# A convolution with max pooling on one core: turned weight taps as neighbours in one row, joint maxima and copies of two images over one PSUM tile, first casts on ScalarE, a last step in two row groups, and a new order

## The chip, the core and the metric

The kernel runs on one core of a Trainium2 chip. The time is the device time of one execution in microseconds, as the median over several runs. A profile of one execution gives the span from the first to the last instruction and what each engine did in it. Engines are named as the profile names them: PE (TensorE), DVE (VectorE), ACT (ScalarE), POOL (GpSimd), SP (SyncE).

## What is computed

`x` is 16 images of 64 channels of 64 x 64 float32 values, `weight` is 128 x 64 x 3 x 3. The result is the 3 x 3 convolution with padding of one pixel, followed by the maximum over each 2 x 2 square:

```python
x_pad = np.pad(x, ((0, 0), (0, 0), (1, 1), (1, 1)))
conv[b, co] += weight[co, ci, kh, kw] * x_pad[b, ci, kh:kh+64, kw:kw+64]   # over ci, kh, kw
output[b, c, i, j] = np.max(conv[b, c, 2*i:2*i+2, 2*j:2*j+2])              # 16 x 128 x 32 x 32
```

## The kernel before

**Work.** Two images lie side by side on the 128 partitions (64 channels each). A step is one pair of images and a quarter of the output rows: 8 output rows of 64 columns before the maximum over columns, for both images, so 32 steps in all (`TYPES`, line 37). Image `h` (0 or 1) of a step uses partitions 64h to 64h+63 on the input side, so the products of image 0 and image 1 use the two row halves of the PE array and run side by side. One product is three matmuls (the taps `kw` = 1, 0, 2, function `taps`, lines 188 to 209) of up to 64 x 512 elements into one of eight PSUM accumulators of 512 float32 values per partition, which is one bank (line 61). A product of image 0 is always interleaved with a product of image 1 (`lanes`, lines 251 to 259): three matmuls of each, in turn. This text calls such a group of six matmuls a slot.

**Two kinds of step.** With c0 and c1 the convolution of an even and the following odd row, each step forms a part that both share and takes the maximum of the rest, so that the maximum over rows is taken before the shared part is added. A K step has five products: PA1 and PA2 into accumulator `ta`, PB1 and PB2 into `tb`, PR (the shared part) into `tb` after the maximum. A W step has four: P2 and P0 into `ta`, P3 into `tb`, P1 (shared) into `tb` after the maximum. A W step starts `tb` from a copy of `ta` (SE, line 404).

**What the other engines do for a step.** Per image: EV (line 395) copies `ta` out of PSUM to SBUF on ACT, MX (line 425) puts the maximum of `tb` and that copy back into `tb` on DVE, then the shared product is added by PE, OD (line 429) copies the odd columns of `tb` to SBUF on ACT, CM (line 433) takes the maximum of the even columns and that copy on DVE and frees `tb`. After the second image's CM a store of both images is issued on SP. Of a W step, D (line 337) and mostly E (line 328) are row differences on POOL, WS (line 310) is a row sum on DVE; KS (line 297) is that of a K step. L and LK load input.

**Order.** The order of every instruction is written out by hand in the string `ORDER` (lines 493 to 547): `MX.4.1` is MX of step 4, image 1. Each engine works through its own instructions in that order. A tile framework puts semaphore waits between engines wherever one instruction reads or writes what another writes or reads. The queues are in order: an instruction that waits holds all that stand behind it on its engine.

**The start.** The weights arrive as [128, 576] and are cast and combined into slots of 64 columns of `wq` (g0, g1, g2, D0, D2, GS, GM, GP). PE turns each two neighbouring slots into one 128 x 128 block (`turn`, T...), and a copy brings the blocks from PSUM to `wt` (`turn_out`, V...). Seven groups have four slots each with a zero or a copied slot (`ring`, u..., on POOL) between, 25 turns in all (lines 133 to 186). The first rows of x are cast on DVE (XEa, XOa, XEb, XOb, line 450). The first K step and first W step run in row halves (F.k.part and G.k.part; Ea, Eb on DVE, Da, Db on POOL make the differences for G). Eight matmuls on a constant (line 551) stand at the very start.

**The end.** The last step, 31, is a W step. Its two images are stored apart, one on ACT's queue and one on SP's (lines 443 to 445).

Of the kernel before, what the change touches and what calls it, by code (L numbers as in the profile page):

```python
# [11 lines left out]
def kernel(  # L12
# [25 lines left out]
    DIFF_ON_VECTOR = (3, 4, 6, 11,)  # L38
    CAST_ON_VECTOR = ()
    SUM_BY_REDUCTION = (1, 3, 9, 11, 12, 14, 16, 17, 19, 20, 22,)  # L40
# [9 lines left out]
    d_pool = ctx.enter_context(tc.tile_pool(name="d_pool", bufs=5))  # L50
    e_pool = ctx.enter_context(tc.tile_pool(name="e_pool", bufs=5))
# [3 lines left out]
    od_pool = ctx.enter_context(tc.tile_pool(name="od_pool", bufs=6))  # L55
    o_pool = ctx.enter_context(tc.tile_pool(name="o_pool", bufs=6))
# [4 lines left out]
    acc = [psum.tile([128, R, W], FP32, name=f"acc_{i}") for i in range(8)]  # L61
# [5 lines left out]
    sbuf_op = [None]  # L67

# [64 lines left out]
    BLOCKS = {"D2": 1, "G0": 5, "D0": 9, "G2": 13, "GM": 17, "G1": 21, "GP": 25}  # L133
    D2, G0, D0, G2, GM, G1, GP = BLOCKS.values()
    RING = ("GM", "G1", "GP")
    wq = const.tile([CO, 29, CI], BF16)
    wt = const.tile([128, 28, CO], BF16)
    gsum = const.tile([CO, 3, CI], FP32)
    for s in range(0, GM, 4):
        nc.gpsimd.memset(wq[:, s, :], 0.0)  # L140
# [8 lines left out]
    def ring(m):  # L149
        s = BLOCKS[m]  # L150
        nc.gpsimd.tensor_copy(out=wq[:, s + 3, :], in_=wq[:, s, :])  # L151

    def turned_cols(m):
        lo = BLOCKS[m] - (m not in RING)
        hi = BLOCKS[m] + 3
        tp = acc[turned[m]].rearrange("p a b -> p (a b)").bitcast(BF16)
        return lo, hi, tp[:, 0 : (hi - lo) * CO]
# [12 lines left out]
    def turn_out(m):  # L170
        free.append(turned[m])
        lo, hi, src = turned_cols(m)
        dst = wt[:, lo:hi, :].rearrange("p a b -> p (a b)")
        if m == "GM":
            nc.scalar.mul(dst, src, 0.5)
        elif m == "GP":
            nc.vector.tensor_scalar_mul(out=dst, in0=src, scalar1=0.5)
        elif m in ("G0", "G2"):
            nc.scalar.copy(out=dst, in_=src)
        else:  # L180
            nc.vector.tensor_copy(out=dst, in_=src)

    def tap_of(m0, kw, half):
        if m0 in (GM, G1, GP):
            return m0 + (kw - half) % 3
        return m0 + kw - half

    def taps(t, h, m0, rows, start=False, skip=None, span=(0, R)):
# [7 lines left out]
        def one(kw):  # L196
            o0, o1, c0, c1 = (0, W, 0, W) if kw == 1 else (1, W, 0, W - 1) if kw == 0 else (0, W - 1, 1, W)
            if start and kw == 1:
# [3 lines left out]
                wt[lo : lo + CI, tap_of(m0, kw, h), :],  # L202
# [18 lines left out]

    def take(where, s, h, fresh=True):
        t = next((t for t in free if fresh or t not in unset), free[0])
        free.remove(t)
        where[s, h] = t
        return t

# [162 lines left out]
    def late_load(s):  # L390
        behind(wload(s), sbuf_op[0])

    ev, od, ot, made = {}, {}, {}, {}

    def evac(s, h):
        ev[s, h] = ev_pool.tile([128, R, W], FP32, name="ev")
# [31 lines left out]

    def odd(s, h):
        od[s, h] = od_pool.tile([128, R, WO], FP32, name="od")  # L430
        nc.scalar.copy(out=od[s, h], in_=acc[tb[s, h]][:, :, 1::2])  # L431

    def colmax(s, h):
        if s not in ot:
            ot[s] = o_pool.tile([128, 2, R, WO], FP32, name="o")
        t = tb.pop((s, h))
# [3 lines left out]
        p, q = place[s]  # L440
        dst = out[2 * p : 2 * p + 2, :, q * R : (q + 1) * R, :].rearrange("b c h w -> c b (h w)")
        src = ot[s].rearrange("p b h w -> p b (h w)")
        if s == N - 1:
            store = nc.scalar if made[s] == 1 else nc.sync
            store.dma_start(out=dst[:, h : h + 1], in_=src[:, h : h + 1])
        elif made[s] == 2:
            nc.sync.dma_start(out=dst, in_=src)


    def cast_rows(lo, hi):  # L450
        on_vector(nc.vector.tensor_copy(out=kx[0][:, lo:hi:2, :], in_=kfirst[:, lo:hi:2, :]))  # L451

    def cast_more(first):
# [15 lines left out]
        "XOa": lambda: cast_rows(1, kmid),  # L469
        "XOb": lambda: cast_rows(kmid, khi),  # L470
        "XEa": lambda: cast_rows(0, kmid),
        "XEb": lambda: cast_rows(kmid + 1, khi),
# [10 lines left out]
        "KS": ks, "WS": ws, "E": we, "D": wd, "L": wload, "LB": late_load, "LK": lk,  # L483
        "SE": seed, "EV": evac, "MX": rowmax, "OD": odd, "CM": colmax,
    }
    for m in BLOCKS:
        steps["u" + m] = lambda m=m: ring(m)
        steps["T" + m] = lambda m=m: turn(m)
        steps["V" + m] = lambda m=m: turn_out(m)
    for m in PRODUCTS:  # L490
# [3 lines left out]
        D0 g2 g1 TD0 TG2 g0 D2 XEa PR.0.1 TD2 VG2 PA1.2.1 VD0 TG0 uG1 TG1 GS F.2.0 VD2 XOa LB.3 LB.4 LB.6  # L494
        LB.8 LB.9 GM VG0 F.3.0 XOb F.0.0 uGM F.1.0 VG1 F.0.1 TGM PA2.2.1 XEb LK.0.0 F.1.1 F.2.1 F.3.1 VGM GP
        Ea KS.0 Eb EV.0.1 G.0.0 EV.0.0 G.0.1 uGP P2.3.1 SEa.0 SEa.1 SEb.1 MX.0.1 Da Db TGP SEb.0 MX.0.0 VGP
        LK.0.1 X2 PR.0.0 G.1.0 X1 G.2.0 PB1.2.1 PB2.2.1 WS.1 G.2.1 G.1.1 L.11 P0.3.1 PA1.2.0 PA2.2.0 P3.3.1
        OD.0.0 OD.0.1 EV.1.0 KS.2 E.3 CM.0.1 EV.1.1 P1.1.1 D.3 CM.0.0 PR.2.1 PB1.2.0 P2.3.0 MX.1.0 PB2.2.0
        EV.2.1 P1.3.1 SE.3.1 EV.2.0 WS.3 MX.1.1 P1.1.0 SE.3.0 P0.3.0 MX.2.0 MX.2.1 EV.3.1 PR.2.0 EV.3.0 D.4
        MX.3.1 OD.2.0 PA1.5.1 OD.1.0 E.4 PA1.5.0 PA2.5.0 P3.3.0 OD.1.1 OD.2.1 L.12 L.14 PA2.5.1 OD.3.1  # L500
        P2.4.1 CM.1.1 CM.2.0 P2.4.0 CM.1.0 PA1.7.1 D.6 EV.5.0 CM.3.1 CM.2.1 MX.3.0 PA2.7.1 PB1.5.1 SE.4.0
        PA1.7.0 PA2.7.0 EV.5.1 SE.4.1 EV.7.0 PB2.5.1 P0.4.1 P0.4.0 P2.6.1 KS.7 E.6 P3.4.1 WS.4 WS.6 P1.3.0
        EV.4.0 PR.5.1 KS.5 WS.8 EV.7.1 P0.6.1 PB1.5.0 PB1.7.0 PB2.5.0 PB2.7.0 L.16 P1.4.1 EV.4.1 MX.5.1
        P3.4.0 OD.3.0 SE.6.1 MX.5.0 LK.1.0 LK.1.1 CM.3.0 MX.4.1 P3.6.1 OD.5.1 PB1.7.1 MX.7.0 PB2.7.1 PR.5.0
        OD.5.0 P2.6.0 EV.6.1 E.8 PR.7.0 MX.4.0 OD.4.1 OD.7.0 CM.5.1 D.8 P1.4.0 SE.6.0 OD.4.0 CM.5.0 E.9
        MX.6.1 CM.7.0 CM.4.0 P1.6.1 P2.8.0 CM.4.1 D.9 P2.8.1 SE.8.0 P0.6.0 P2.9.1 MX.7.1 P3.6.0 OD.6.1
        EV.6.0 P0.8.0 L.17 P3.8.0 SE.8.1 CM.6.1 PR.7.1 EV.8.0 OD.7.1 P0.8.1 MX.6.0 SE.9.1 E.11 MX.8.0 P1.6.0
        D.11 CM.7.1 P2.9.0 OD.6.0 EV.8.1 CM.6.0 WS.9 P3.8.1 P1.8.0 P0.9.1 PA1.10.1 SE.9.0 P2.11.0 OD.8.0
        L.19 L.20 P3.9.1 PA2.10.1 KS.10 EV.9.1 SE.11.0 P0.9.0 CM.8.0 E.14 P2.11.1 MX.9.1 P3.9.0 MX.8.1
        P0.11.0 EV.9.0 EV.10.1 MX.9.0 P1.9.1 D.14 E.12 P1.8.1 PA1.10.0 P3.11.0 PA2.10.0 SE.11.1 OD.9.1  # L510
        P1.9.0 P2.14.0 WS.11 CM.9.1 P0.11.1 P3.11.1 EV.11.0 EV.11.1 OD.8.1 OD.9.0 EV.10.0 P1.11.0 PA1.13.0
        PA1.13.1 MX.11.0 MX.11.1 PA2.13.1 D.12 L.22 L.23 PA2.13.0 P2.12.0 CM.8.1 CM.9.0 D.16 P1.11.1 EV.13.1
        P2.12.1 OD.11.0 SE.14.0 OD.11.1 PB1.10.1 WS.14 P0.14.0 CM.11.0 PB2.10.1 P3.14.0 CM.11.1 L.24 P0.12.0
        SE.12.1 P0.12.1 SE.12.0 P3.12.1 P3.12.0 EV.14.0 PB1.10.0 P2.14.1 WS.12 PB2.10.0 EV.13.0 MX.10.1
        EV.12.1 MX.14.0 E.16 EV.12.0 MX.12.1 PR.10.1 P1.14.0 MX.12.0 SE.14.1 OD.10.1 P1.12.0 PB1.13.1
        PA1.18.0 KS.15 KS.13 CM.10.1 P0.14.1 MX.10.0 OD.14.0 P3.14.1 CM.14.0 EV.14.1 P1.12.1 PR.10.0
        PB2.13.1 WS.16 MX.13.1 PA2.18.0 PA1.15.1 PA2.15.1 PR.13.1 OD.10.0 MX.14.1 PB1.13.0 OD.12.1 EV.18.0
        LK.2.0 P1.14.1 PB2.13.0 P2.16.0 CM.10.0 L.25 PA1.15.0 OD.12.0 EV.15.1 OD.13.1 CM.12.1 PA2.15.0
        SE.16.0 CM.13.1 P0.16.0 CM.12.0 L.27 L.28 P3.16.0 MX.13.0 P2.16.1 D.17 PR.13.0 PB1.15.0 PB1.15.1
        E.17 D.20 E.20 D.19 PB2.15.1 PB2.15.0 SE.16.1 EV.15.0 WS.17 P0.16.1 MX.15.1 P3.16.1 EV.16.0 OD.14.1  # L520
        PR.15.1 P2.17.1 MX.16.0 P1.16.0 EV.16.1 OD.13.0 MX.16.1 OD.15.1 SE.17.1 CM.14.1 P1.16.1 P2.20.1
        CM.13.0 CM.15.1 OD.16.0 PA1.21.0 P2.17.0 MX.15.0 P0.17.1 PR.15.0 E.23 E.19 CM.16.0 P3.17.1 OD.16.1
        CM.16.1 SE.20.1 EV.17.1 P0.20.1 P3.20.1 WS.20 PA2.21.0 P2.19.0 OD.15.0 SE.17.0 P3.17.0 EV.20.1
        MX.17.1 CM.15.0 P1.17.1 E.24 P0.17.0 WS.22 PA1.21.1 SE.19.0 P0.19.0 OD.17.1 EV.21.0 MX.20.1 CM.17.1
        D.22 EV.17.0 PA2.21.1 EV.21.1 EV.19.0 P3.19.0 P2.19.1 MX.17.0 KS.18 P2.23.0 P1.17.0 WS.19 P1.20.1
        PA1.18.1 P0.19.1 SE.19.1 MX.19.0 PB1.18.0 OD.17.0 OD.20.1 PA2.18.1 PB2.18.0 EV.19.1 P1.19.0 CM.20.1
        D.23 CM.17.0 MX.18.0 E.22 P3.19.1 PB1.18.1 SE.23.0 P2.20.0 EV.18.1 MX.19.1 PB2.18.1 PR.18.0 P1.19.1
# [66 lines left out]
```

## Time and profile before

| what | value |
|---|---|
| median of 3 runs | 104.69 us (104.35 to 105.06) |
| the profiled execution's own time | 105.15 us |
| span of that execution | 103.4 us |
| outside the span | 1.75 us |
| busy: PE, DVE, ACT, POOL | 97.2, 92.0, 82.2, 75.6 us |
| first weight turn on PE, first product on PE | 4.40 us, 6.46 us |
| first matmul of PR.29, the third slot from the end | 96.13 us |
| last matmul of all begins | 98.30 us |
| last store is issued | 99.82 us |
| mean granted PE clock | 0.993 |

The profiled execution took 0.46 us more than the median of the runs, so a time that is summed against the profile is brought to the median by taking 0.46 us off. Busy time of PE counts pipelined matmuls, whose ends are modelled; the starts of the matmuls are the better clock. In a steady stretch a slot of six matmuls takes 0.645 us from its first start to the next slot's first start (PR.0.0 begins at 11.025 us, the next slot at 11.670 us).

### The profile page before, as it was taken

What the parts mean: (1) busy time and instruction counts of PE and PEld (TensorE: products, weight loads), DVE (VectorE), ACT (ScalarE), POOL (GpSimd) and SP (SyncE); (2) the same over time, 40 slices, a digit from 0 to 9 for tenths busy, and PEclk for the clock granted to TensorE, in tenths of its full rate; (3) what the DMA queues carried; (4) which work ended last, traced back from release to release, by engine and by line L of the source; (5) the groups of instructions that cost most, each with busy time, mean ns of one, the idle gap of its engine ahead of it and who ended that gap; (6) DMA issues with size and microseconds to landing.
All of it is one profiled execution on the core that took longest, in us unless ns stands there. A gap on an engine that the chain in (4) does not pass through costs nothing.

```text
span 103.4 us, 2541 instructions
## 1 busy us (share of the span) xinstructions
PE 97.2 (94%) x909; PEld 62.9 (61%) x909; DVE 92.0 (89%) x179; ACT 82.2 (79%) x181; POOL 75.6 (73%) x65
## 2 busy tenths in 40 slices
PE   6999799999999999999999999999999999999910
PEld 2497655555865465576666685556746777777600
DVE  1389899999999999999999999999989996979960
ACT  4546988886789997993887898987899898698820
POOL 6046869773995899998999997959997919970000
PEclk9999999999999999999999999999999999999997
DMA  2988999999999999999859992187699232006152
GB/s 62 299 312 262 360 291 268 349 416 404 248 194 298 286 318 339 351 340 204 163 159 261 312 384 101 56 205 263 176 154 257 81 136 101 0 13 233 65 202 102
DMA packets 13341, 23.33 MB, mean 226 GB/s; under 512 B 1040, under 2 KB 9488, under 8 KB 13328
## 3 DMA queue, kind: packets, MB, share of 16 engines
q1 hardware_dynamic: 12320, 20.68, 60.8%
q0 software_dynamic: 864, 2.36, 13.7%
q8 instruction: 7, 0.11, 0.4%
q10 hardware_dynamic: 144, 0.13, 0.4%
q14 instruction: 6, 0.05, 0.1%
HBM read 17.14 MB, written 8.39 MB: 247 GB/s over the span
## 4 chain that ended last, share of the span: by engine, by line
PE 91%; DVE 3%; issue 1%; DVEq 0%
PE acc L200 85%; PE acc L551 3%; PE acc L164 2%; DVE acc L427 2%; DVE o L437 1%; DVEq L589 0%; DVEq L437 0%; DVEq L427 0%
## 5 line engine op out<-in xcount | busy, mean ns | idle before, releaser
L200 PEld LDWEIGHTS <-wt 64*128 64x128 bf16 x876 | 59.6, 94 | 31.5 <-issue 1.5
L341 POOL TENSOR_TENSOR wd<-wx 128x1024 bf16<-128x1024 f32 x20 | 47.1, 2361 | 7.7 <-PE acc L200 3.4
L200 PE MATMUL acc<-wd,wt 64*128 64x504 bf16 (+3 forms) x264 | 50.1, 367 | 0.0
L200 PE MATMUL acc<-kx,wt 64*128 64x504 bf16 (+6 forms) x288 | 50.0, 356 | 0.0
L427 DVE TENSOR_TENSOR acc<-acc,ev 128x512 f32<-128x512 f32 x64 | 42.0, 691 | 1.1 <-ACT ev L401 0.3
L200 PE MATMUL acc<-we,wt 64*128 64x512 bf16 (+2 forms) x132 | 31.7, 367 | 0.0
L200 PE MATMUL acc<-ws,wt 64*128 64x504 bf16 (+1 forms) x126 | 28.7, 377 | 0.1
L401 ACT ACTIVATE ev<-acc 128x512 f32<-128x512 f32 x42 | 25.1, 608 | 2.7 <-PE acc L200 2.3
L431 ACT COPY od<-acc 128x256 f32<-128x256 f32 x64 | 22.5, 379 | 5.8 <-PE acc L200 5.2
L437 DVE TENSOR_TENSOR o<-acc,od 128x256 f32<-128x256 f32 x64 | 24.5, 416 | 2.1 <-ACT od L431 1.9
L411 ACT COPY acc<-acc 128x512 f32<-128x512 f32 x40 | 23.0, 581 | 3.0 <-PE acc L200 1.7
L332 POOL TENSOR_TENSOR we<-wx 128x512 bf16<-128x512 f32 x16 | 20.2, 1273 | 3.3 <-DVE ws L323 2.4
L200 PE MATMUL acc<-ks,wt 64*128 64x504 bf16 (+1 forms) x66 | 16.5, 377 | 0.5 <-DVE acc L427 0.5
L315 DVE TENSOR_REDUCE ws<-wx 128x512 bf16<-128x1024 f32 x11 | 13.5, 1229 | 0.0
L399 ACT COPY ev<-acc 128x512 f32<-128x512 f32 x22 | 12.9, 595 | 0.6 <-PE acc L200 0.6
L323 DVE TENSOR_TENSOR ws<-wx 128x512 bf16<-128x512 f32 x10 | 7.1, 723 | 0.0
L301 DVE TENSOR_TENSOR ks<-kx 128x512 bf16<-128x512 bf16 x11 | 4.6, 429 | 0.3 <-ACT kx L458 0.3
L551 PE MATMUL acc<-const-bfloat16-1.0 128*128 128x512 bf16 x8 | 3.6, 628 | 0.8 <-PEq L575 0.8
L95 POOL DMA_DIRECT2D kx<-in_x_dram x6 | 3.5, 587 | 0.7 <-DVE kx L451 0.7
L164 PEld LDWEIGHTS <-wq 128*128 128x128 bf16 x25 | 2.3, 132 | 1.4 <-issue 1.4
L151 POOL COPY wq<-wq 128x64 bf16<-128x64 bf16 x3 | 0.7, 241 | 3.1 <-ACT wq L462 2.5
L164 PE MATMUL acc<-ident,wq 128*128 128x128 bf16 x25 | 2.8, 285 | 0.0
(30 smaller groups left out, 22.3 us busy)
## 6 DMA issues: line engine op xcount, KB each, us to landing
out_dram<-o SPq DMA_DIRECT2D x31, 256.0 KB, 4.2
wx<-in_x_dram SPq DMA_DIRECT2D x10, 512.0 KB, 7.2
wx<-in_x_dram SPq DMA_DIRECT2D x5, 544.0 KB, 7.6
wx<-in_x_dram SPq DMA_DIRECT2D x5, 480.0 KB, 7.4
kx<-in_x_dram POOLq DMA_DIRECT2D x2, 528.0 KB, 7.4
ksecond<-in_x_dram SPq DMA_DIRECT2D x1, 512.0 KB, 7.0
kx<-in_x_dram POOLq DMA_DIRECT2D x2, 256.0 KB, 7.0
kx<-in_x_dram POOLq DMA_DIRECT2D x1, 496.0 KB, 12.0
```

The costliest lines, as they stand in the source:

```text
L164: nc.tensor.transpose(tp[:, (j - lo) * CO : (j - lo + 1) * CO], wq[:, j : j + 2, :].rearrange("a b c -> a (b c)"), ident,)
L200: nc.tensor.matmul(acc[t][:, i0:i1, o0:o1], wt[lo : lo + CI, tap_of(m0, kw, h), :], rows(lo, i0, i1, c0, c1), start=start and kw == 1, sto ...
L315: nc.vector.tensor_reduce(out=row["ws", s], in_=t[:, f : f + 2 * R, :].rearrange("p (r two) w -> p r w two", two=2), axis=mybir.AxisListTy ...
L323: nc.vector.tensor_tensor(out=row["ws", s], in0=t[:, f : f + 2 * R : 2, :], in1=t[:, f + 1 : f + 2 * R : 2, :], op=ADD)
L332: inst = (nc.vector if vector else nc.gpsimd).tensor_tensor(out=row["we", s], in0=t[:, f : f + 2 * R : 2, :], in1=t[:, f + 1 : f + 2 * R : ...
L341: nc.gpsimd.tensor_tensor(out=row["wd", s], in0=t[:, f + 1 : f + 1 + 2 * R, :], in1=t[:, f - 1 : f - 1 + 2 * R, :], op=SUB)
L399: nc.scalar.copy(out=ev[s, h], in_=acc[t])
L401: nc.scalar.mul(ev[s, h], acc[t], -1.0)
L411: nc.scalar.copy(out=acc[t], in_=acc[ta[s, h]])
L427: nc.vector.tensor_tensor(out=t, in0=t, in1=ev[s, h], op=MAX)
L431: nc.scalar.copy(out=od[s, h], in_=acc[tb[s, h]][:, :, 1::2])
L437: nc.vector.tensor_tensor(out=ot[s][:, h], in0=acc[t][:, :, 0::2], in1=od[s, h], op=MAX)
```

## The change

**Taps in one row.** `wq` has 25 slots and `wt` 24 blocks. The order of the groups is D0, G2, D2, G0, G1, GM, GP with no slot between the first five, so that a block that turns the last slot of one group turns the first slot of the next one too. 24 turns; no copied slots (`ring` is gone).

**Joint operations of two images.** All eight accumulators become one PSUM tile `bank` of eight banks. For steps in three lists, one instruction covers both images, through the view `bank[:, a : b + 1 : b - a]` of the two banks a and b. MM is the joint MX, OO the joint OD, CC the joint CM. Where image 0's bank has the higher number the joint form falls back to two single ones.

**First casts** XEa, XEb, XOa, XOb move from DVE to ACT; VG1 goes from DVE to ACT; VG2 and VGM from ACT to DVE. The late loads wait for the last cast.

**The last step** adds its shared product in two row groups (Z.0, Z.1), copies and maxes each group and image by itself (OZ.part.image, CZ.part.image) and stores each group for both images on SP's queue.

**Order and buffers.** `ORDER` is written anew. `d_pool` goes from 5 to 4 buffers, `e_pool` from 5 to 6, `od_pool` 6 to 4, `o_pool` 6 to 5; `ev2_pool` (3), `od2_pool` (3) and `last_pool` (4) are new. Which steps take their difference on DVE and their row sum by a reduction changes, their numbers (4 and 11) do not.

```diff
-    DIFF_ON_VECTOR = (3, 4, 6, 11,)
+    DIFF_ON_VECTOR = (3, 9, 16, 22,)
+    SWAPPED = ("VG1", "VG2", "VGM", "XEa", "XEb", "XOa", "XOb",)
+    JOINT_ROWMAX = (0, 1, 10, 11, 30,)
+    JOINT_ODD = (1, 2, 3, 5, 8, 10, 11, 14, 15, 27, 29, 30,)
+    JOINT_COLMAX = (0, 1, 2, 5, 8, 11, 12, 15, 21, 24, 29, 30,)
...
-    acc = [psum.tile([128, R, W], FP32, name=f"acc_{i}") for i in range(8)]
+    bank = psum.tile([128, 8, R, W], FP32, name="bank")
+    acc = [bank[:, i] for i in range(8)]
...
-    BLOCKS = {"D2": 1, "G0": 5, "D0": 9, "G2": 13, "GM": 17, "G1": 21, "GP": 25}
+    BLOCKS = {"D0": 1, "G2": 4, "D2": 7, "G0": 10, "G1": 13, "GM": 17, "GP": 21}
...
+    def both(s):
+        a, b = tb[s, 0], tb[s, 1]
+        return bank[:, a : b + 1 : b - a]
...
+    def rowmax_both(s):
+        if tb[s, 0] > tb[s, 1]:
+            rowmax(s, 0)
+            rowmax(s, 1)
+            return
+        nc.vector.tensor_tensor(out=both(s), in0=both(s), in1=ev2[s], op=MAX)
...
+    def odd_both(s):
+        if tb[s, 0] > tb[s, 1]:
+            odd(s, 0)
+            odd(s, 1)
+            return
+        od_tile(s, 0)
+        od_tile(s, 1)
+        nc.scalar.copy(out=od2[s], in_=both(s)[:, :, :, 1::2])
...
+    def colmax_both(s):
...
+        nc.vector.tensor_tensor(out=ot[s], in0=both(s)[:, :, :, 0::2], in1=od2[s], op=MAX)
+        free.extend((tb.pop((s, 0)), tb.pop((s, 1))))
+        store(s)
...
+    def last_product(part):
+        s = N - 1
+        m0, of = (GP, "ws") if TYPES[s] == "W" else (G1, "ks")
+        pair_of_taps(tb, s, m0, step1(row[of, s]), False, None, span_of(part))
...
+    def cast_rows(name, lo, hi):
+        dst, src = kx[0][:, lo:hi:2, :], kfirst[:, lo:hi:2, :]
+        if name in SWAPPED:
+            gate[0] = nc.scalar.copy(out=dst, in_=src)
+        else:
+            gate[0] = on_vector(nc.vector.tensor_copy(out=dst, in_=src))
```

The start and the end of the new order, and a piece of it (`...` marks what is left out):

```
D0 g2 g0 TD0 g1 D2 GS VD0 TG2 TD2 XEa TG0 VG2 TG1 XOa LB.3 ... F.2.0 XOb VG0
F.0.0 F.0.1 GM XEb GP KS.0 F.1.0 TGM F.1.1 EV.0.0 LK.0.0 VGM Ea F.3.0 F.2.1 Eb F.3.1 ...
VG1 Da G.0.0 G.0.1 MM.0 SEa.0 SEa.1 Db X1 TGP VGP G.1.0 G.2.0 SEb.1 SEb.0 ...
...
P2.3.0 PB1.2.0 EV.2.1 EV.2.0 MM.1 PB1.2.1 PB2.2.1 PB2.2.0 L.11 WS.3 SE.3.0 P1.1.0 P1.1.1 E.4 MX.2.1
MX.2.0 SE.3.1 P0.3.1 P0.3.0 OO.1 P3.3.0 P3.3.1 CC.1 E.6 D.4 EV.3.1 PR.2.0 ...
...
P0.31.1 EV.31.0 P3.31.1 PR.29.0 EV.31.1 MX.31.0 P1.30.0 P1.30.1 MX.31.1 OO.29
OO.30 CC.29 Z.0 Z.1 OZ.0.1 OZ.1.1 CC.30 OZ.1.0 CZ.0.1 OZ.0.0 CZ.1.0 CZ.1.1 CZ.0.0
```

In the built program, counting the increments of each semaphore tells which instruction a wait is for. The joint operations whose two banks are not neighbours, and waits before and behind them. In the built program these treat a joint operation as one that touches every bank from a to b; only a wait marked "its own" is for a bank that both instructions use:

| joint operation | its banks | it waits for | PE slot that waits for it |
|---|---|---|---|
| MM.1 (DVE) | 0, 7 | P2.3 (bank 2), EV.2.0 (bank 4) | PB1.2.1 (bank 5) |
| OO.1 (ACT) | 0, 7 | P0.3 (bank 2), MX.2.0 (bank 5) | P3.3.1 (bank 1) |
| CC.1 (DVE) | 0, 7 | P3.3.1 (bank 4) | PR.2.1 (bank 5) |
| OO.3 (ACT) | 1, 4 | PA2.5.1 (bank 3) | PB1.5, through CM.3.0 and CM.3.1 |
| OO.5 (ACT) | 1, 4 | MX.4.1 (bank 2) | P1.4.0 (bank 3) |
| CC.5 (DVE) | 1, 4 | P1.4.0 (bank 3) | P2.6.0 (bank 2) |
| CC.8 (DVE) | 3, 5 | P1.9.0 (bank 4) | P2.12.1 |
| MM.11 (DVE) | 1, 3 | PA1.10.0 (bank 3, its own) | P2.12.0 (bank 2) |
| CC.11 (DVE) | 1, 3 | P3.12.1, EV.12.0 (bank 2) | PA2.18.0 (bank 1, its own) |
| MM.10 (DVE) | 0, 5 | PB2.13.1 (bank 1), OO.14 (2, 3) | PA2.15.0 (bank 4) |
| OO.10 (ACT) | 0, 5 | CM.14.0 (bank 2) | P3.16.0 (bank 3) |
| OO.15 (ACT) | 0, 7 | MX.17.1 (bank 1) | PA1.21.0 (bank 4) |
| CC.15 (DVE) | 0, 7 | P2.17.0 (bank 6) | PA2.21.0 (bank 4) |
| OO.27 (ACT) | 1, 6 | MX.26.1 (3), PB1.26.0 (4) | P3.28.1 (bank 5) |
| OO.29, then CC.29 | 0, 4 | MX.31.1 (bank 1) | Z.0 (bank 1) |

The joint operations on neighbouring banks (MM.0, CC.0, OO.2, CC.2, CC.12, OO.14, MM.30, OO.30, CC.30) have no such waits. CC.21 and CC.24 fall back to single ones.

## Prediction

> **What bounds the kernel now.** I read the page first: which engine is busy, and where in the span.
>
> ```profile
> PE 97.2 (94%) x909; PEld 62.9 (61%) x909; DVE 92.0 (89%) x179; ACT 82.2 (79%) x181; POOL 75.6 (73%) x65
> ...
> PE   6999799999999999999999999999999999999910
> ...
> PEclk9999999999999999999999999999999999999997
> ...
> PE 91%; DVE 3%; issue 1%; DVEq 0%
> ```
>
> PE carries 91% of the chain that ended last, at full clock. DVE, at 89%, has some slack, and a joint operation that only saves DVE time saves nothing by itself. The chain in order of time shows where PE is not the reason:
>
> ```profile
> 0.78 3.57 PE acc L551 x8
> ...
> 4.40 2.12 PE acc L164 x19
> 6.52 1.67 PE acc L200 x30
> ...
> 9.68 1.31 DVE acc L427 x2
> 10.98 0.04 issue
> 11.03 64.89 PE acc L200 x609
> 75.92 0.03 issue
> 75.94 20.43 PE acc L200 x186
> ...
> 97.72 0.69 DVE o L437 x2
> ```
>
> From 11.03 to 96.4 PE runs slot behind slot; the gaps between matmul starts there add up to 0.86 us. So whatever makes PE wait in this stretch is added to the time almost whole. What is left outside is the start (6.46 us to the first product, a wait of 0.54 us at 10.49) and the end, from the last matmul to the last store. Third, the durations by line, and last the timeline at both ends:
>
> ```profile
> L427 DVE TENSOR_TENSOR acc<-acc,ev 128x512 f32<-128x512 f32 x64 | 42.0, 691 | 1.1 <-ACT ev L401 0.3
> ...
> L431 ACT COPY od<-acc 128x256 f32<-128x256 f32 x64 | 22.5, 379 | 5.8 <-PE acc L200 5.2
> L437 DVE TENSOR_TENSOR o<-acc,od 128x256 f32<-128x256 f32 x64 | 24.5, 416 | 2.1 <-ACT od L431 1.9
> ...
> L399 ACT COPY ev<-acc 128x512 f32<-128x512 f32 x22 | 12.9, 595 | 0.6 <-PE acc L200 0.6
> ```
>
> ```profile
> 5.51 0.36 DVE L451 CAST kx<-kfirst 128x320 bf16<-128x320 f32 x1 [0.84 <-DMA kfirst<-in_x_dram]
> ...
> 9.64 2.50 POOL L368 TENSOR_TENSOR wd<-wx 128x512 bf16<-128x512 f32 x2 [0.38 <-DVE we L353]
> ...
> 97.72 2.07 DVE L437 TENSOR_TENSOR o<-acc,od 128x256 f32<-128x256 f32 x6
> ...
> 99.82 0.34 SPq L445 DMA_DIRECT2D out_dram<-o  x1
> ```
>
> Three hand-overs are read from starts and ends in the same trace: from the end of a PE slot to ACT or DVE 0.20 us (39 starts of ACT), from DVE or ACT to PE 0.05, ACT to DVE 0.03, DVE to ACT 0.09.
>
> **The start.** Before, 19 turns at 0.107 us run from 4.40 to 6.43 and the first product starts at 6.46. Now 16 turns stand ahead of it: 4.40 + 16 x 0.107 = 6.11. Its other inputs: VD0 after TD0, 5.05 + 0.41 = 5.46; XEa now on ACT at the landing, 5.5, with 0.36 to 0.48 (1.2 us for two 512-element casts, L458, by size) until 5.95. So the first product comes 0.3 us earlier. The next inputs follow in time (XOb, then VG0, end at about 6.9 on ACT, where F.1.0 is due at 7.1). The half products end near 9.8 instead of 10.05. Then G.1.0 waits for Da on POOL, behind Eb, behind the landing of wx near 8.9: 8.9 + 0.48 + 1.27 + 0.1 = 10.75. PR.0.0 has gone behind it, so the 0.54 us wait of before moves there. Before reaches the same amount of product work at 12.97, the new order at 12.71: -0.26 us. Between -0.5 (the turns saved whole) and +0.5 (Db late too); I take -0.26. The earlier gate lets the late loads go 0.7 us sooner behind the first ones on the same queue: nothing. Three POOL copies (3 x 0.24) go; POOL waits there, nothing.
>
> **The joint operations.** Extrapolated from 416 ns at 256 and 691 ns at 512 elements, MM at 1024 takes 0.69 + 2 x 0.275 = 1.24 us, where a pair of MX takes 0.60 + 0.69 = 1.29 (L427 pairs start 0.60 apart). CC takes 0.69 against 0.33 + 0.42. So each saves DVE or ACT 0.06 us, under 1 us on DVE and ACT each: off PE's path, nothing. The Trainium skill, Perfetto Trace Analysis, section Optimizing Scalar/DVE Operations, gives about 125 ns of overhead per DVE instruction on PSUM and says that grouping helps a saturated engine; by it 15 joint maxima would save 1.9 us of DVE, which here lies beside PE as well. (Two of the 17 maxima, CC.21 and CC.24, fall back to single ones.) The same section says that breaking up instructions helps where they cause bubbles on other engines, and that is the side this case is on, as follows.
>
> What costs is the waits. Where banks a and b are not neighbours, the built program has PE wait for the joint operation although PE's slot uses another bank, and the joint operation wait for the PE slot just before. Then PE must run empty: slot end, 0.20, the operation, 0.05, less 0.645 for each slot that stands between. The prices of an empty round are 0.20 + 1.24 + 0.05 = 1.50 for MM, 0.20 + 0.60 + 0.05 = 0.85 for OO, 0.20 + 0.69 + 0.05 = 0.95 for CC (sums of the unrounded terms).
>
> - Step 1: P2.3 | MM.1 | PB1.2, P0.3 | OO.1 | P3.3, P3.3 | CC.1 | PR.2, no slot between in any: 1.50 + 0.85 + 0.95 = 3.30.
> - Step 3: PA2.5, OO.3, CM.3.0, CM.3.1, PB1.5, with two slots between: 0.20 + 0.60 + 0.03 + 0.42 + 0.33 + 0.05 - 1.29 = 0.34.
> - Step 5: OO.5 waits for MX.4.1, which DVE reaches 4.98 us after CM.3.1 (WS 1.15, two KS 0.35, two MX 0.60, WS 0.64, MX 0.60 and 0.69); with OO.5 and hand-overs 5.64, and PE has seven slots for it, 4.57: 1.07. Then CC.5 with no slot between: 0.95. Together 2.02.
> - Step 8: P1.9 | CC.8 | P2.12: 0.95.
> - Step 11: MM.11 with one slot between, 1.50 - 0.645 = 0.85; OO.11, EV.12.0 and CC.11 in a row with two slots between, 0.20 + 0.49 + 0.60 + 0.03 + 0.69 + 0.05 - 1.29 = 0.77. Together 1.62.
> - Step 10: MM.10, no slot between, 1.50; OO.10 with one, 0.85 - 0.645 = 0.20. Together 1.70.
> - Step 15: MX.17.1 and OO.15 with one slot between, 0.20 + 0.69 + 0.09 + 0.60 + 0.05 - 0.645 = 0.98; CC.15, none between, 0.95. Together 1.93.
> - Step 27: PB1.26 | OO.27 | P3.28: 0.85.
>
> Sum 12.7 us. No row of before shows a joint operation; the bounds are half of it, 6.4 (ACT and DVE, which gain time while PE stands, take the operation up sooner than its order lets me count), and 12.7 + 14 x 0.35 = 17.6, if every round meets a queue as MM.1 does: EV.2.0, for which it waits, stands on ACT behind EV.1.1, EV.1.0 and EV.2.1, 0.49 each, some 0.35 us too late by my count of the start. I take the sum, since empty rounds can't be shorter than their terms.
>
> **The end.** Let p be the start of PR.29, 96.13 before. MX.31.1 waits for that slot: p + 0.645 + 0.20, ends p + 1.55. OO.29 (box of banks 0 to 4) waits for it, ends p + 2.24; CC.29 ends p + 2.96; Z.0 (bank 1) waits for CC.29: p + 3.01, where P1.31 began at p + 1.74 before. Z.0 and Z.1, six pairs of 0.11: p + 3.67. All OZ wait for the last matmul of Z.1, p + 3.87, so the two groups do not overlap. ACT copies of 128 elements, by size 0.27 and 0.16 apart: the fourth ends p + 4.62. CZ.1.0 waits for that; CZ.1.1 ends p + 5.13, CZ.0.0 p + 5.33; the first store takes SP some 0.37, the second begins p + 5.53. Before, the last store is issued at 99.82 - 96.13 = p + 3.69. So +1.84, between 0.6 (if only the two tails differ) and 2.5. What follows a store, 3.56 us to the end of the span, stays. On the two groups the Trainium skill, PSUM — Partial Sum Buffer, section PSUM bank collisions raise a hardware error, speaks against the change: two engines must not touch one bank at a time, so semaphores guard whole banks, and OZ.0 can't run while Z.1 writes the same bank. Without that rule OZ.0 could begin 0.33 us, one half slot, sooner; the built program's wait agrees with it.
>
> **Other edits.** D, E, WS and KS are as many as before; with PE slower, POOL (75.6 us) and the loads have more slack than before, so the smaller `d_pool` and the moved loads and stores are hidden behind PE; if that cover were gone, a late D would cost what D.24 costs now, 0.27 us of idle PE at 75.9. The small waits of before, 0.86 us, I leave in the sum, as the new order has its own.
>
> **Sum.** 105.15 - 0.26 + 12.71 + 1.84 = 119.44 against the profiled execution; less 0.46, 119.0 us as a median.
>
> **Rivals.**
> - Half covered (12 in 100): the joint operations are mostly done when PE comes. For it speaks that DVE and ACT have 11% and 21% of slack; against it that in eight places no slot stands between. 119.0 - 6.35 = 112.6.
> - Dearer rounds (13): each meets a queue on DVE or ACT. For it, MM.1 and OO.5; against it, that idle PE lets the others catch up. 119.0 + 4.9 = 123.9.
> - The clock falls (4): gaps in PE's work bring back the half clock of the start, where 512 columns take 3.57 / 8 = 0.446 us against 0.215 later. If each of the three clusters (steps 1 to 5, 8 to 10, 15) lost half of the 5.6 us that the start takes to full clock, 8.4 us: 127.4. Against it: the 0.54 us wait at 10.49 left the clock at 1.00. The Trainium skill, TensorE: Matmul & The Clock Gate, section A second HAM failure mode, tells of short idle times between groups of matmuls that make the clock swing; the trace shows none yet.
> - Not slower (5): the waits cost nothing. That decides if at each place PE has two slots, 1.29 us, queued ahead of the wait. Then what is left is -0.26 at the start and the 0.37 us that P1.31's second matmul waits ahead of 97.87: 104.69 - 0.63 = 104.1. Against it, the table of waits: most have no slot between.
>
> **How the numbers follow.** The forecast has 66 chances in 100, and its own range is 116 to 122. 114 to 124 takes in about half of the cheaper and most of the dearer case and leaves out under 2 in 10. A measurement of this kernel can tell about 1% from no change. Faster by over 1% and within 1% come from the case of 104.1 alone: 0.03 and 0.02; slower 0.95.
>
> **What would show it.** Right: PE's first product near 6.1; idle PE of about 1.5 us ahead of PB1.2 (for MM.1) and PA2.15 (for MM.10), 0.9 ahead of P3.3, PR.2, P2.6, P2.12, PA1.21, PA2.21, P3.28; 1.7 ahead of Z.0's second matmul; waits of PE for the new OO, MM and CC lines in the list of waits; PE's busy share down by 10 points. Wrong: PE gaps of under 0.3 us there, or MM well off 1.24 us.

## The result, and the profile after

The changed kernel takes 121.18 us (median of 6 runs, 120.63 to 121.55), the kernel before 104.63 us beside it (104.25 to 105.08): a ratio of 1.157 (95% interval 1.152 to 1.162). The forecast was 119.0 us. The profiled execution of the changed kernel took 121.39 us, with a span of 119.6 us.

The page of the changed kernel, the same lines as shown of before: busy times, PE and its granted clock in 40 slices, and the chain's shares.

```profile
PE 101.3 (85%) x914; PEld 54.4 (45%) x914; DVE 93.7 (78%) x163; ACT 81.2 (68%) x174; POOL 74.7 (62%) x61
...
PE   7999947799679997798959967999999999899520
...
PEclk9999999999999999999999999999999999999975
...
PE 34%; DVE 3%; ACT 2%; issue 0%; DVEq 0%; ACTq 0%
```

PE's row has dents where before had nines: at steps 1 to 5 (the 6th to the 12th slice), steps 8 to 15 (the 16th to the 25th) and at the end. The clock row has none there, and between the dents the matmuls keep their spacing of 0.215 us, so PE is idle, not slow. DVE and ACT are busy for about as many us as before (92.0 and 82.2), over a longer span. What PE waited for is in the list of waits of PE alone (us in total, times, longest). Before, the list has one entry behind the start:

```profile
PE acc L200 <- DVE acc L427: 0.5, 1, 0.5
```

and after it has the three joint operations: CC, MM and OO in this order.

```profile
PE bank L204 <- DVE o L504: 4.9, 6, 1.6
PE bank L204 <- DVE bank L455: 4.0, 3, 1.7
PE bank L204 <- ACT od L472: 3.4, 5, 0.9
```

These 12.3 us are counted from modelled ends of matmuls. By the starts of matmuls (how much more than 0.215 us lies between the later matmul of one pair and that of the next) PE stands 14.0 us at the joint operations of steps 1 to 27 and 1.7 us at the last one. One round of the timeline, around MM.1 (start, duration, engine and line; in brackets the idle time before and who ended it):

```profile
14.33 0.90 PE L204 MATMUL bank<-we,wt 64*128 64x512 bf16 x6
...
14.53 1.07 ACT L420 COPY ev<-bank 128x512 f32<-128x512 f32 x2 [0.16 <-PE bank L204]
...
15.64 1.23 DVE L455 TENSOR_TENSOR bank<-bank,ev 128x1024 f32<-128x1024 f32 x1 [1.14 <-ACT ev L420]
...
16.93 0.83 PE L204 MATMUL bank<-kx,wt 64*128 64x512 bf16 x6 [1.69 <-DVE bank L455]
```

P2.3 starts at 14.33. DVE is idle for 1.14 us until ACT has copied EV.2.1 and EV.2.0, works MM.1 for 1.23 us, and PE's next slot starts 0.06 us after its end. In the built program it is the matmul of PB1.2.0, into bank 5, that waits for it (the table ahead names this slot by PB1.2.1); MM.1 uses banks 0 and 7.

To split the time, three marks are read in each kernel's trace: the first matmul of PA1.2 (the start is over), the first of PR.29, and the end of the last maximum over columns.

| profiled execution | PA1.2 begins at | from there to PR.29 | from PR.29 to the last maximum's end |
|---|---|---|---|
| before | 12.98 | 83.14 | 3.67 |
| after | 13.03 | 97.65 | 5.55 |
| neighbours only | 12.34 | 83.44 | 4.11 |
| step 1 joint | 12.30 | 87.38 | 4.13 |
| step 29 joint | 12.72 | 83.44 | 5.45 |
| middle joint | 12.99 | 93.79 | 4.21 |
| waits without joint | 12.49 | 87.57 | 4.11 |
| none joint | 13.09 | 83.42 | 4.11 |
| old end | 12.62 | 83.44 | 3.69 |
| one tile | 12.87 | 83.14 | 3.65 |
| new start | 12.36 | 83.16 | 3.67 |

After against before: 0.05 at the start, 14.51 in the middle, 1.88 at the end, and 0.19 less outside these marks (5.16 against 5.35): 16.25 of the 16.24 us between 121.39 and 105.15.

### The profile page after: what moved, and what is told of

Its sections match the earlier page's. It is cut to its first block, busy times and chain, and to the rows that moved or that the text cites. A ratio compares the mean times of both kernels' runs of the same rounds, so it can differ in the third digit from the quotient of the medians.

```text
span 119.6 us, 2527 instructions
## 1 busy us (share of the span) xinstructions
PE 101.3 (85%) x914; PEld 54.4 (45%) x914; DVE 93.7 (78%) x163; ACT 81.2 (68%) x174; POOL 74.7 (62%) x61
## 5 line engine op out<-in xcount | busy, mean ns | idle before, releaser
L204 PE MATMUL bank<-wd,wt 64*128 64x504 bf16 (+3 forms) x264 | 53.4, 367 | 1.9 <-ACT od L472 1.6
L204 PE MATMUL bank<-kx,wt 64*128 64x504 bf16 (+6 forms) x288 | 50.3, 356 | 4.8 <-DVE bank L455 3.1
L448 DVE TENSOR_TENSOR bank<-bank,ev 128x512 f32<-128x512 f32 x54 | 36.0, 692 | 1.7 <-PE bank L204 0.7
L204 PE MATMUL bank<-we,wt 64*128 64x512 bf16 (+3 forms) x132 | 31.8, 367 | 2.0 <-DVE o L504 1.1
L432 ACT COPY bank<-bank 128x512 f32<-128x512 f32 x40 | 23.1, 583 | 12.6 <-DVE o L504 4.3
L204 PE MATMUL bank<-ws,wt 64*128 64x512 bf16 (+3 forms) x132 | 28.6, 367 | 3.1 <-DVE o L504 2.2
L422 ACT ACTIVATE ev<-bank 128x512 f32<-128x512 f32 x42 | 24.9, 606 | 4.8 <-PE bank L204 2.7
L492 DVE TENSOR_TENSOR o<-bank,od 128x256 f32<-128x256 f32 x42 | 16.5, 419 | 4.4 <-ACT od L476 2.2
L204 PE MATMUL bank<-ks,wt 64*128 64x504 bf16 (+1 forms) x66 | 14.5, 377 | 0.9 <-DVE o L504 0.9
L476 ACT COPY od<-bank 128x256 f32<-128x256 f32 x38 | 13.5, 382 | 2.1 <-DVE o L504 1.2
L455 DVE TENSOR_TENSOR bank<-bank,ev 128x1024 f32<-128x1024 f32 x5 | 6.2, 1233 | 2.9 <-ACT ev L420 1.6
```

What stands on the lines that cost most here:

```text
L204: nc.tensor.matmul(acc[t][:, i0:i1, o0:o1], wt[lo : lo + CI, m0 + kw - h, :], rows(lo, i0, i1, c0, c1), start=start and kw == 1, stop=True ...
L422: nc.scalar.mul(ev[s, h], acc[t], -1.0)
L432: nc.scalar.copy(out=acc[t], in_=acc[ta[s, h]])
L448: nc.vector.tensor_tensor(out=t, in0=t, in1=ev[s, h], op=MAX)
L492: nc.vector.tensor_tensor(out=ot[s][:, h], in0=acc[t][:, :, 0::2], in1=od[s, h], op=MAX)
```

## The experiments

Theory A is that of the prediction: a joint operation on two banks that are not neighbours is guarded as if it touched every bank between, and PE stands empty for it. The kernel before, beside the experiments, was at 104.87, 104.80 and 105.00 us in the three groups of runs.

**Joint only on neighbouring banks.** In `rowmax_both`, `odd_both` and `colmax_both`:

```diff
-        if tb[s, 0] > tb[s, 1]:
+        if tb[s, 1] - tb[s, 0] != 1:
```

> The changed kernel, with a joint operation only where image 1's bank is the next one after image 0's (nine places stay joint: MM.0, MM.30, CC.0, CC.2, CC.12, CC.30, OO.2, OO.14, OO.30), two single operations elsewhere. Theory A (the wait on all banks between a and b is the cost): PE's empty rounds go with the joint operations, 14 to 15 us of idle PE by the trace of the changed kernel, and the wait of Z.0 for CC.29, 1.7 us, with them; 121.2 less 15 to 16.5 gives 104.5 to 106.5 us. Rival B (the new order, the smaller pools, the first casts and the two-group end are the cost, and the joint operations only show where the time was going to be lost anyway): most of the idle time comes back behind single operations, over 115 us.

105.48 us, 1.006 (1.004 to 1.008) of before. PE's list of waits, behind the eight matmuls on a constant, holds only the last step and the start:

```profile
PE bank L204 <- DVE bank L448: 0.2, 1, 0.2
PE bank L204 <- ACT bank L444: 0.2, 1, 0.2
```

15.7 of the 16.5 us are gone with the 18 joint operations on banks that are not neighbours (the table ahead leaves out two of them, OO.8 and OO.11); order, pools, casts and the new end are all still there. Rival B is out.

**Step 1 joint again.** The same, with `and s != 1` in the three conditions.

> As the kernel with joint operations on neighbouring banks only, but step 1's three (MM.1, OO.1, CC.1 on banks 0 and 7) are joint again. Theory A: the kernel with neighbours only plus 3.3 us by the prediction's terms (1.50 + 0.85 + 0.95) to 4.0 us by the idle PE that the changed kernel's trace shows ahead of PB1.2.1, P3.3.1 and PR.2.1 (1.95 + 0.97 + 1.03), and idle PE of these sizes at these three places alone. Rival B: within 1 us of the kernel with neighbours only.

109.57 us, 1.047 (1.043 to 1.051): 4.09 more than with neighbours only; 3.94 in the trace's middle. PE's waits show the three operations, once each:

```profile
PE bank L204 <- DVE bank L455: 1.7, 1, 1.7
PE bank L204 <- DVE o L504: 0.8, 1, 0.8
PE bank L204 <- ACT od L472: 0.8, 1, 0.8
```

By matmul starts (the earlier matmul of each pair) they are within 0.01 us of those in the changed kernel, 1.95, 0.97 and 1.03 us. Rival B is out here too.

**The waits without the joint operation.** Neighbours only, and step 1's single operations get the joint ones' waits (`behind` adds a wait of one instruction for another; `mx` is the MX ahead of the pair).

```diff
+    def boxed(op, s):
+        mx = last.get("MX")
+        first, second = op(s, 0), op(s, 1)
+        if s == 1:
+            behind(first, last["PE"])
+            if op is rowmax:
+                behind(first, last["EV"])
+            if op is odd:
+                behind(first, mx)
+            last["hold"] = second
...
-            nc.tensor.matmul(
+            last["PE"] = nc.tensor.matmul(
...
+            behind(last["PE"], last.pop("hold", None))
```

> As the kernel with joint operations on neighbouring banks only, so step 1's operations on banks 0 and 7 are single, but with the waits of the joint ones put in as explicit ones: the first of MX.1 waits for PE's last matmul ahead of it and for EV.2.0, the first of OD.1 for P0.3 and MX.2.0, the first of CM.1 for P3.3.1, and PE's next matmul each time for the second of the pair. Theory A (the waits alone are the cost): as with step 1's joint operations, 109.6 us, plus 0.06 us for each pair that takes longer than the joint operation, 109.4 to 110.1. Rival E (the long operation over two far banks is the cost, by its length or by its access): as with neighbours only, 105.5 us.

109.44 us, 1.046 (1.043 to 1.049), as with the joint operations (109.57). In the timeline two single MX stand where MM.1 stood, and PE waits as long:

```profile
15.10 1.30 DVE L461 TENSOR_TENSOR bank<-bank,ev 128x512 f32<-128x512 f32 x2 [1.14 <-ACT ev L422]
...
16.45 1.25 PE L205 MATMUL bank<-kx,wt 64*128 64x512 bf16 x10 [1.76 <-DVE bank L461]
```

This is the run that settles the cause at step 1: neither the length of the joint operation nor its reach over far banks costs anything that shows; the waits do. Rival E is out. For the other steps, where no such run was made, the cause is the same by what goes and comes with their joint operations.

**One PSUM tile, nothing joint.** The kernel before with `bank` and `acc = [bank[:, i] for i in range(8)]`.

> The kernel before with its eight accumulators as slices of one PSUM tile and no joint operation. Theory A: the waits come from a joint operation's own view, not from the common tile, so as the kernel before, 104.2 to 105.1 us. Rival C (one tile alone makes waits between operations on different banks, so the joint form only adds to it): over 106 us.

104.79 us, 0.9995 (0.997 to 1.002). The common tile alone makes no waits; rival C is out.

**Middle joint.** The changed kernel with the joint operations of steps 1 and 29 apart: `if tb[s, 0] > tb[s, 1] or tb[s, 1] - tb[s, 0] != 1 and s in (1, 29):`

> The changed kernel with step 1's and step 29's joint operations single and all others as in it: so the far joint operations of steps 3, 5, 8, 10, 11, 15 and 27 (twelve at eleven waits of PE) are left. Theory A, three ways: by the prediction's terms 9.41 us (0.34 + 2.02 + 0.95 + 1.70 + 1.62 + 1.93 + 0.85) above the 105.48 us with neighbours only, so 114.9; by the idle PE that the changed kernel's trace shows ahead of those slots, 10.75 us, so 116.2; by what the changed kernel (121.18) has left when step 1 (4.09) and step 29 (1.41) are taken off as measured alone, if the places add up, 115.7. Rival H (the places do not add up: once one round has stopped PE, DVE and ACT catch up and the next ones cost less or more): off 115.7 by more than 1 us.

(Thirteen far operations are left, not twelve: OO.8 is one too; PE stands less than 0.1 us for it.) 115.59 us, 1.101 (1.098 to 1.105), within 0.1 us of what is left when steps 1 and 29 are taken off as measured alone. The three groups (step 1, the middle, step 29) add up: 105.48 + 4.09 + 10.11 + 1.41 (the next run) = 121.09, against 121.18. Rival H is out: PE's idle time in one group buys nothing in the next. Whether the places inside the middle help one another, this does not show. The way that gave 116.2 was too high, because its 10.75 us takes the longer of the two images' waits at every place, which counts a shift between them twice; by the later matmul of each pair it is 10.2 us.

**Step 29 joint.** Neighbours only with `and s != 29` in the conditions.

> As the kernel with joint operations on neighbouring banks only, but step 29's two (OO.29 and CC.29 on banks 0 and 4) are joint again. Theory A: Z.0's second matmul, which starts 0.05 us after MX.31.1 ends in the kernel with neighbours only, starts 1.39 us after it in the changed kernel (112.50 to 113.89), so 1.34 us more than 105.48: 106.8 us (106.4 to 107.2). Rival: the last copies and maxima catch up with it, under 106.0 us.

106.89 us, 1.021 (1.018 to 1.023): 1.41 more; the rival is out. The chain that ended last, in the changed kernel (start, duration, what):

```profile
111.79 0.71 DVE bank L448
112.51 0.02 issue
112.53 0.59 ACT od L472
113.12 0.02 issue
113.15 0.70 DVE o L504
113.85 0.04 issue
113.89 0.83 PE bank L204 x11
```

and with neighbours only, where PE takes up Z.0 behind MX.31.1 itself:

```profile
96.80 0.71 DVE bank L448
97.51 0.04 issue
97.55 0.83 PE bank L204 x11
```

**The old end.** Neighbours only, with P1.31, OD.31 and CM.31 as before and the two images stored on two queues; the copies and maxima of step 30 are single again too, and those of steps 29 and 30 stand in the order of before.

```diff
-OO.29 OO.30 CC.29 Z.0 Z.1 OZ.0.1 OZ.1.1 CC.30 OZ.1.0 CZ.0.1 OZ.0.0 CZ.1.0 CZ.1.1 CZ.0.0
+OD.29.1 OD.29.0 P1.31.1 CM.29.0 CM.29.1 P1.31.0 OD.30.1 CM.30.1 OD.30.0 OD.31.0 OD.31.1 CM.30.0 CM.31.0 CM.31.1
```

> As the kernel with joint operations on neighbouring banks only, but with the end of the kernel before: the last step's shared product in one piece, its two images stored apart on two queues. In the trace with neighbours only, the last maximum ends 4.11 us after PR.29 begins (95.78 to 99.89), in the kernel before 3.67 us after it (96.13 to 99.80). If the two row groups cost what these differ by, 0.44 us less than the 105.48 us with neighbours only, so 105.0 us (104.7 to 105.3). Rival: the two groups cost nothing since the store that follows is smaller, 105.5 us.

105.17 us, 1.005 (1.002 to 1.007): 0.31 less than with neighbours only by the medians, whose intervals overlap. In the traces the last maximum ends 0.42 us sooner behind PR.29 (4.11 to 3.69), the span only 0.19 us sooner (7.48 to 7.30), so the rival is half right: behind the smaller last store less time follows. The two row groups bring nothing, and the trace shows that all four OZ start only behind the last matmul of Z.1 (its end 98.36, the first OZ 98.40 us, with neighbours only); that this alone is what they cost is not shown.

**No joint operation at all.**

> The changed kernel with no joint operation at all: two single ones at all 27 places, so the nine on neighbouring banks are apart too. By the prediction's step (0.05 to 0.06 us of DVE or ACT for each joint operation, off PE's path) the time stays within 0.3 us of the 105.48 us with neighbours only. Rival F (a joint operation on neighbouring banks saves time on the path): 106 us or more. Rival G (it costs time even there, since both images' slots must be done before it starts): 105.0 us or less.

105.60 us, 1.006 (1.003 to 1.009), as with neighbours only. So the nine joint operations that cost nothing bring nothing either, and rivals F and G are out. Their gain in DVE's and ACT's time can be read from the two traces, joint and single ones taken together: MX and MM are busy for 41.96 us with nine joint and for 42.09 with none, CM and CC for 23.39 and 23.66, OD and OO for 21.09 and 21.28. With 2, 4 and 3 joint operations that is 0.06 to 0.07 us each, what the prediction had counted (0.06). The Trainium skill, Perfetto Trace Analysis, section Optimizing Scalar/DVE Operations, puts the overhead of a DVE instruction on PSUM at about 125 ns; joining two saved about half of that here.

**The new start alone.** The kernel before with the 24 turns, the casts on ACT and the changed kernel's order up to F.3.1.

> The kernel before with the changed kernel's start alone: taps in one row, 24 turns, first casts on ScalarE, the changed kernel's order up to F.3.1, from there the order of before. By the prediction's step on the start: first product 0.35 us earlier, the end 0.26 us earlier, so 104.4 us with a range of 104.1 to 105.1. Rival D (the start is worse than counted, since casts on ScalarE delay the copies of the turned taps and Da waits for a later Eb): 105.2 us or more.

104.75 us, 0.9992 (0.997 to 1.001): no difference from the kernel before that these runs can tell. Rival D is out; the forecast gain of 0.26 us is neither shown nor excluded. No version beat the kernel before by more than its interval.

## Why the prediction was right, and what it had too small

It named the waits on all banks from a to b as the cause, and the runs bear it out: without the joint operations on far banks 15.7 us go, and at step 1 the waits alone, with no joint operation, take the same time as with it. By its steps (idle PE in the changed kernel, between the later matmul of one pair and that of the next; the last row by the prediction's own mark):

| step | forecast | measured |
|---|---|---|
| 1 (MM, OO, CC) | 3.30 | 1.86 + 0.95 + 1.02 = 3.83 |
| 3 | 0.34 | 0.38 |
| 5 (OO, CC) | 2.02 | 1.07 + 0.99 = 2.06 |
| 8 | 0.95 | 1.00 |
| 11 (MM, CC) | 1.62 | 1.06 + 0.74 = 1.80 |
| 10 (MM, OO) | 1.70 | 1.56 + 0.47 = 2.03 |
| 15 (OO, CC) | 1.93 | 1.05 + 0.97 = 2.02 |
| 27 | 0.85 | 0.88 |
| sum | 12.71 | 14.0 |
| end (start of the last store) | 1.84 | 2.15 |

With neighbours only the middle is 14.21 us shorter (97.65 against 83.44), so the sum of the places holds to 0.2 us. It must be taken along the same matmul of each pair: at CC.5, CC.8, CC.11 and OO.27 a matmul of image 0 goes ahead of the wait that stops image 1, and the two images stand at different places.

Every gap that the prediction listed is there, and the steps rank as forecast, with 10 and 15 level. Most are a little too small. The durations are not the reason (three groups of the changed kernel: MM 1233 ns where 1.24 us was worked out, OO 587 for 0.60, CC 688 for 0.69):

```profile
L472 ACT COPY od<-bank 128x512 f32<-128x512 f32 x12 | 6.9, 587 | 8.5 <-DVE bank L448 4.6
L504 DVE TENSOR_TENSOR o<-bank,od 128x512 f32<-128x512 f32 x10 | 6.8, 688 | 7.5 <-PE bank L204 4.1
L455 DVE TENSOR_TENSOR bank<-bank,ev 128x1024 f32<-128x1024 f32 x5 | 6.2, 1233 | 2.9 <-ACT ev L420 1.6
```

Two terms were mis-sized. The larger is a queue that the sum put at nothing, at three of the fourteen places: MM.1, MM.11 and OO.10 stand 0.36, 0.21 and 0.26 us over their forecasts, 0.83 of the 1.3 us that are missing here. The sum lets an operation start when the PE slot ahead of it has ended, 0.645 + 0.20 = 0.845 us after that slot's first start. MM.1 began 1.31 us after P2.3, 0.03 behind the end of EV.2.0 on ACT (the upper bound had 0.35 for this). MM.11 began 1.41 us after PA1.10.0, 0.13 behind the end of CM.9.0, which stands ahead of it on DVE. OO.10 began 0.11 us behind the end of CM.14.0, which DVE finished only 1.72 us after MM.10, behind three other operations. This is what the rival of dearer rounds named; it had all rounds meet a queue, and three did. The time, 121.18, lies about halfway between the forecast of 119.0 and that rival's 123.9, but only 0.8 us of the way is queues.

The smaller term is "slot end, 0.20" itself: where 0.845 us had been counted it was 0.98 at OO.1, 0.93 at CC.1, 0.95 at MM.10 and 0.88 at CC.15.

All terms together: the forecast was 119.44 us against the profiled execution, and 121.39 came, 1.95 more.

- The middle is 1.80 of it (14.51 for 12.71). By the comparison with neighbours only 1.50 are the joint operations (14.21 for 12.71). The other 0.30 is the new order, which was put at nothing (83.44 with neighbours only against 83.14; PE is late there by 0.14 to 0.27 us at D.16, SE.20.0, SE.23.1 and D.24, where before it is late by 0.26 at D.24 and 0.15 at D.25).
- The start is 0.31: put at -0.26 us, it came to +0.05 by the marks, and its first product came at 6.25 us instead of 6.1.
- The end is 0.31 by the prediction's mark: the last store starts 5.84 us behind PR.29, before 3.69. Most of this was there at MX.31.1, which ended 1.81 us behind PR.29 where 1.55 had been counted. The prediction left what follows that store at 3.56 us; it came to 3.08, which gives 0.48 back. To the last maximum the end's 1.88 is 1.34 for the wait on CC.29, 0.44 for the two groups, and 0.10 by which MX.31.1 starts later behind PR.29.

The medians are 2.2 us apart, 0.25 more, since this profiled execution lies 0.21 us above its median and 0.46 had been taken off.

What the other rivals said: not slower is out by 17 us. Half covered is out, since no place came in clearly below its forecast. For a falling clock, the granted clock is 1.00 in each stretch from 13 to 103 us with all these gaps in it, and, which says more, the first matmuls behind the gap at MM.1 (1.95 us by the earlier matmul of the pair) are spaced 0.215 us as ever. The Trainium skill, TensorE: Matmul & The Clock Gate, section A second HAM failure mode, tells of a clock that swings when PE idles between groups of matmuls; here idle times of up to 1.95 us, three of them between 15 and 22 us, did not move it.

One thing happened that the prediction did not speak of: ACT's SE copies wait for far joint operations too (4.3 us in total for CC, 1.3 for MM.1). At step 1 it costs nothing, as the run with explicit waits on MX, OD and CM alone shows: there SE.3.0 runs ahead of MX.1 (14.95 against 15.10 us), and PE loses the same time. For the other steps this is not shown.

## What to carry to other kernels

Where one instruction takes in two buffers through a strided view, ask the built program what its range covers: here the range from the first to the last bank was guarded, and most of the joint operations on far banks became barriers for PE at 0.4 to 1.9 us a piece, while joining itself was worth 0.07 us at best. Price such a barrier as an empty round (slot end to operation, operation, operation to PE, less the slots that can run between) and add the places up; the three groups tested here did not help one another. Then look what stands ahead of the operation on its own engine: that was the larger part of what this forecast missed. On neighbouring buffers the joint operations cost PE nothing, and brought nothing either; an engine that bounds the time could use the 0.06 us, but here DVE and ACT did not bound it.

## What the runs showed that was not expected

The start differs by up to 0.8 us between the profiles of the nine kernels that have the changed one. The 16 turns in the changed kernel's profile and in that of the new start alone:

```profile
4.45 1.86 PE L171 MATMUL bank<-ident,wq 128*128 128x128 bf16 x16
```

```profile
4.52 1.22 PE L162 MATMUL acc<-ident,wq 128*128 128x128 bf16 x16 [0.38 <-DVE wq L464]
```

In the first, each turn but the second starts 0.107 us after the one before, in the second 0.055 to 0.057, but for one wait of 0.21 us. Of the eleven profiles, three keep 0.107 through all of these first turns (before, after, middle joint), four have 0.055 from the first one on, and four change on the way. With the changed kernel's start, PA1.2 begins at 12.99 and 13.03 us in the two that stay slow, at 12.30 to 12.72 in the four that are fast from the first, and at 12.34 to 13.09 in the three that change, with the same or nearly the same instructions ahead of it. The granted clock is shown as 1.00 in all of these stretches, so that column does not tell of it; the spacing of the matmul starts does. The prediction priced a turn at 0.107 us; where it takes 0.056, three turns less save half as much. What sets the moment of the change is left open.
